# Hybrid DeltaNet and forgetting-attention trunk: later modulation strips, and an output projection whose second half gets its operands ahead of other loads

## The chip, the cores and the metric

The kernel runs on one core of a Trainium2 chip. The metric is the device time of one execution in microseconds (us).

## The reference

Two layers of width 1024 over 1024 tokens, in float32. Layer 0 mixes tokens by a gated delta rule (DeltaNet) with a short causal convolution, layer 1 by forgetting attention. Each layer normalizes its input and modulates it with a shift and a scale from a condition vector c; its result is multiplied by a gate, also from c.

```
cond = jax.nn.silu(c)
for i in range(DEPTH):                                   # DEPTH = 2
    mod = cond @ ada_w[i] + ada_b[i]                     # (1024) x (1024, 3072)
    shift, scale, gate = jnp.split(mod[:, None, :], 3, axis=-1)
    h = rmsnorm(x, norm_w[i]) * (1 + scale) + shift
    if i == 0:
        y = gdn_mixer(h, ...)     # input projection, conv, 16 heads of 128, ..., o @ w_out (2048 -> 1024)
    else:
        y = fox_mixer(h, ...)     # 16 heads of 64, softmax with a forget bias, gate, o @ w_out
    x = x + gate * y
return rmsnorm(x, final_norm_w)
```

## The kernel before

Float32 products are made from three matmuls on split operands: a rounded high part and the rest as low part (`mm3`; ScalarE writes the high part, VectorE or GpSimd subtracts for the low part). Tokens are in two halves of 512, and tiles of 128.

**The order of work.** TensorE's order is written out by hand. Generators (one for each strand of work) yield a delay, and a small planner, `Flow`, always advances the live one with the lowest priority number whose time has come; its clock adds the modelled cost of each matmul. What the other engines and the DMA queue do follows from the order in which work is emitted and from when its inputs and buffers are planned to be ready; each engine, and the queue on SyncE (SP) that issues all the DMAs here, then takes its list strictly in order. A tile of a pool is used again in rotation, and its next writer waits for the last reader.

**Layer 0** runs in 16 units, 8 groups of two heads for each token half (index `i`, `ts[i]`). A unit projects k, q and two v tiles and the z tiles (`proj_tile`), and then goes through the inversion of its triangular matrix (with DMA round trips through `lb`, `lr`, `rb` and `rmat`) and the chain of state updates. `done["kp"]` counts finished k tiles. Results go split to `og_d` and `ogl_d` in DRAM, 16 heads by 1024 tokens. In the units of the first half the weights are split and the parts stored to DRAM; in the second half most come back from there.

**Modulation strips.** The shift, scale and gate for layer 1, and the gate of layer 0, are made by `ada_all` in eight strips of 512 columns (`ada_strip`): eight loads of 128 x 512 into the two buffers `nx`, a multiply-add on VectorE for each, and a few matmuls into a bank of the ring `mm` (two PSUM banks, shared with the projections). `hold(lambda: done["kp"] >= AD0 + 1)` sets the unit with which they begin, and a copy of a piece of `ts[AD0]["k"]` into `nx` (L1283) ties the loads to that data.

**The output projection of layer 0** (`out_proj_a`) goes over token halves `h`, pairs of token tiles `tp`, column halves (in the first token half only) and 16 heads `k`. Weights come three steps ahead (`wnext`), are loaded to a third of `ht_h` (L433) and split to `whi` and `wlo`. The operands are read back from `og_d` and `ogl_d`, one head at a time (`ohi`, `olo`, L450, `out_o`), or, in the second token half after the first OX = 4 heads, two heads at a time (`yh`, `yl`, L461, `out_pair`), kept in the list `oq` in advance. The old x (`xs`, L507) is added at the end of a pair, and the new x is written to `x1_d` (L526).

**The second stage** begins, in the order of emission, when the chain of layer 0 is done: its memory takes the place of that of the units. While the second half of the projection runs, `norm2` goes through the eight token tiles (for the first four, x1 is read back into `v`, L1372, normalized into `wraw`, transposed on TensorE and split into `h2_h`, `h2_l`; the last four come from `n2read` without a reload), and `preload` fetches and splits the first eight weights of layer 1 through the buffer `kn` (L343). Then come attention and its output projection.

Of the kernel before, what the change touches and what calls it, by code (L numbers as in the profile page):

```python
# [8 lines left out]
F32 = mybir.dt.float32  # L9
# [9 lines left out]
KT = D // P  # L19
# [60 lines left out]
OGW = 2000  # L80
OL = 4
OX = 4
Y_NN = 8000
KPE = (7, 5)
KC = 3
# [3 lines left out]
Y_N2 = 8500  # L89
Y_N3 = 8500  # L90
ADP = 3500
AD0 = 5
R_AD = 600
R_AS = 2500
R_OA = 1150
# [100 lines left out]
def tile_trunk(  # L196
# [24 lines left out]
    nc = tc.nc  # L221
# [124 lines left out]
    def mm3(ps, wh, wl, ah, al, first, last):  # L346
        mm(ps, wh, ah, start=first, stop=False)
        mm(ps, wh, al, start=False, stop=False)
        mm(ps, wl, ah, start=False, stop=last)

    def hold(ok):
        while not ok():
            yield 300
# [10 lines left out]
    def xt_(shape, name, bufs=1, dt=F32):  # L364
        return px.tile(shape, dt, name=name, tag=name, bufs=bufs)

    xdone = {}
    where = {}

    wq, w_src, wcache = [], [], {}  # L370
    oq, o_src = [], []
# [19 lines left out]
    def oload(ahead):  # L391
        while len(oq) < ahead and o_src:
            oq.extend(o_src.pop(0)())

    def wnext(ahead):
        half(2)
        while len(wq) < ahead and w_src and len(set(wid)) < 3:
            wload()
        wid.pop(0)
        return wq.pop(0)  # L400
# [43 lines left out]
    def out_o(k, tok):  # L444
        def load():
            w = 2 * P
            hi = xt_([P, w], "ohi", 4, F32R)
            lo = xt_([P, w], "olo", 4, F32R)
            for v, d in ((hi, og_d), (lo, ogl_d)):
                nc.sync.dma_start(v.bitcast(F32), d[k, :, tok : tok + w])  # L450
            return [(hi, lo)]

        return load

    def out_pair(k, tok):
        def load():
            w = 2 * P
            pr = []
            for n, d in (("yh", og_d), ("yl", ogl_d)):
                v = where["py"].tile([P, 2, w], F32R, name=n, tag=n, bufs=4)  # L460
                nc.sync.dma_start(v.bitcast(F32), d[k : k + 2, :, tok : tok + w].rearrange("k p t -> p k t"))  # L461
                pr.append(v)
            return [(pr[0][:, i], pr[1][:, i]) for i in range(2)]

        return load

    def out_list(h):
        n = (512, D)[h]
        for tp in range(0, CPH, 2):
            for cs in range(0, D, n):  # L470
                w_src.extend(out_w(k, cs, n) for k in range(0, 16, D // n))
                if h:
                    k0 = 0 if tp else OX
                    o_src.extend(out_o(k, h * HALF + tp * P) for k in range(k0))
                    o_src.extend(out_pair(k, h * HALF + tp * P) for k in range(k0, 16, 2))
                else:
                    o_src.extend(out_o(k, tp * P) for k in range(16))

    def out_proj_a():
        gx = xt_([P, 4, D], "ht_h")  # L480
        gb0 = gx[:, 0]
        where["raw"] = [gx[:, i] for i in range(1, 4)]
        for h in range(2):
            n = (512, 1024)[h]
            if h:
                yield from hold(lambda: "bank" in where)
                yield OGW
            xs = xt_([P, CPH, D], "ht_l")
            for tp in range(0, CPH, 2):
                for cs in range(0, D, n):  # L490
                    acc = None
                    for k in range(16):
                        wh, wl = wnext((5, 3)[h])
                        if not h and (tp, cs, k) == (2, D - n, 8):
                            out_list(1)
                        oload((OL, 7)[h])
                        hi, lo = oq.pop(0)
                        if acc is None:
                            acc = []
                            for b in range(2 + 2 * h):  # L500
                                acc.append((yield from (acc_bank if b < 2 else where["bank"])()))
                        if (tp, cs, k) == (0, 0, 2):
                            if h == 0:
                                nc.sync.dma_start(gb0, gate_d[0:1, :].broadcast_to([P, D]))
                            for t in range(CPH):
                                r0 = (h * CPH + t) * P
                                nc.sync.dma_start(xs[:, t], x[r0 : r0 + P, :])  # L507
                        for t in range(2):
                            o = slice(t * P, (t + 1) * P)
                            for c in range(n // 512):  # L510
                                wc = slice(c * 512, c * 512 + 512)
                                mm3(acc[2 * c + t], hi[:, o], lo[:, o], wh[:, wc], wl[:, wc], k == 0, k == 15)
                            if h:
                                yield 0
                        if not h:
                            yield 0
                    for t in range(2):
                        for c in range(n // 512):
                            c0 = cs + c * 512
                            tg = xt_([P, D], "wlo", 5)[:, 0:512]  # L520
                            nc.vector.tensor_tensor(tg, acc[2 * c + t], gb0[:, c0 : c0 + 512], op=ALU.mult)
                            flow.free(acc[2 * c + t], R_OA + 600 * (2 * c + t))
                            xv = xs[:, tp + t, c0 : c0 + 512]
                            nc.gpsimd.tensor_tensor(xv, xv, tg, op=ALU.add)
                for t in range(tp, tp + 2):
                    nc.sync.dma_start(x1_d[h * CPH + t], xs[:, t])  # L526
                    if h:
                        where["n2read"](h * CPH + t, xs[:, t])
                    xdone[h * CPH + t] = flow.t

    with ExitStack() as sa:
# [133 lines left out]
        def norm_tile(xt, jk, evac, part=None):  # L665
# [4 lines left out]
            nc.vector.tensor_scalar(xt, xt, rs, None, op0=ALU.mult)  # L670
            yield Y_NN
            for k0 in range(0, KT, 4):
# [603 lines left out]
        def ada_all():  # L1276
            yield from hold(lambda: done["kp"] >= AD0 + 1)
            def al(shape, name, bufs):
                t = at([P, D], name, bufs) if name == "nx" else at([P, 512], name, bufs)
                return t[0 : shape[0], 0 : shape[1]]  # L1280

            for _ in range(2):
                nc.vector.tensor_copy(al([P, KT], "nx", 2), ts[AD0]["k"][:, 0, 0:KT])  # L1283
            for l, cl in strips:
# [26 lines left out]
    with ExitStack() as sb:  # L1311
# [3 lines left out]
        def bt(shape, name, bufs=1, dt=F32):  # L1315
            pool = pb if name in LEFT else where["p2"]
            return pool.tile(shape, dt, name=name, tag=name, bufs=bufs)
# [11 lines left out]
        h2_l = bt([P, KT, S], "h2_l", 1, F32R)  # L1329
        sy = sb.enter_context(ExitStack())  # L1330
        where["py"] = sy.enter_context(tc.tile_pool(name="py", bufs=1, reuse_waits="tile"))

        def small(sh, n, b=1):
            return pb.tile(sh, F32, name=n, tag=n, bufs=b)
# [27 lines left out]
        def norm2(t):  # L1362
            yield from hold(lambda: t in xdone)
            if t >= CPH:
                yield max(0.0, xdone[t] + Y_N3 + 2500 * (t % 2) - flow.t)
                hf = bt([P, KT, P], "v", 4)
                jk = n2jk[t]
            else:
                yield 2500
                hf = bt([P, KT, P], "v", 4)  # L1370
                xt = hf.rearrange("p k t -> p (k t)")
                nc.sync.dma_start(xt, x1_d[t])  # L1372
                yield 1500
                jk = [bt([P, 512], "wraw", 2) for _ in range(2)]
                scaled(xt, jk)
                yield Y_N2
            for k0 in range(0, KT, 4):
                ps = yield from pst("pt", 2)
                for k in range(4):
                    tr_(ps[:, k * P : (k + 1) * P], jk[k0 // 4][:, k * P : (k + 1) * P], ident)  # L1380
                for k in range(4):
                    kk = k0 + k
                    nc.vector.tensor_scalar(
                        hf[:, kk], ps[:, k * P : (k + 1) * P], gcol[1][:, kk : kk + 1],
                        scol[1][:, kk : kk + 1], op0=ALU.mult, op1=ALU.add,
                    )
                flow.free(ps, R_N)
                yield 0
            tok = slice(t * P, (t + 1) * P)
            split(h2_h[:, :, tok], h2_l[:, :, tok], hf)  # L1390
# [19 lines left out]

        def preload():
            raw = bt([P, 2, 512], "kn")
            for k in range(KT):
                yield Y_PB
                bload(raw[:, k % 2])
# [528 lines left out]
```

## Time and profile before

| | |
|---|---|
| time, median of 3 runs | 1947.3 us (1943.26 to 1947.73) |
| the profiled execution | 1945.78 us, span 1943.8 us |
| granted TensorE clock, mean | 0.971 |
| busy: PE, PE weight load | 1828.4 us (94%), 1524.4 us (78%) |
| busy: DVE, ACT, POOL | 1328.3 us (68%), 1033.3 us (53%), 367.0 us (19%) |
| bytes moved by DMA | 307.16 MB, mean 158 GB/s |
| loads of the strips | 64 of 256 KB, 3.4 us to landing, from 325.7 to 754.0 us |

PE is TensorE's matmuls, PEld its weight loads, DVE VectorE, ACT ScalarE, POOL GpSimd, SP the engine that issues DMAs (SPq its queue). A row of a timeline gives the start in us, the length, the engine, the line of the kernel, the operation, and what it writes from what. In square brackets stands the idle time of that engine just before and what ended it. A row of waits gives the total in us, how often, and the longest. Matmuls are pipelined and their ends are modelled, so two starts tell more than one length. The granted clock is given as a share of full speed.

### The profile page before, as it was taken

To read this page: it belongs to the slowest core of one execution; us is meant where nothing else is said; L and a number is where in the kernel's file an instruction comes from. 1 tells how busy PE (TensorE), PEld (TensorE's weight loads), DVE (VectorE), ACT (ScalarE), POOL (GpSimd) and SP (SyncE) were. 2 spreads that over 40 slices of the span, in tenths; PEclk is the share of its full clock that TensorE was granted. 3 is DMA by queue.
4 is the path that set the end of the run, shared out by engine and by line. 5 is a ranking of instruction groups with operands and counts; after the bars stand their busy time and mean duration, and the time that the engine had idled before them with its cause. 6 is when DMAs were issued, how large, how long until landed. Compare 5 with 4: busy or idle time off the path is not lost.

```text
span 1943.8 us, 35877 instructions
## 1 busy us (share of the span) xinstructions
PE 1828.4 (94%) x12888; PEld 1524.4 (78%) x12888; DVE 1328.3 (68%) x3323; ACT 1033.3 (53%) x2674; POOL 367.0 (19%) x402
## 2 busy tenths in 40 slices
PE   6989999999899999999899799999999999999798
PEld 4767778777787878878776578798988988989576
DVE  5677888788786777776665585475665656656764
ACT  4565566565564555555444453465565555655631
POOL 1100110101210110010001244223223132221222
PEclk7889999899999999999999899999999999999899
DMA  7576767667656565454689982112021011112423
GB/s 270 187 229 205 233 210 245 207 212 249 229 181 186 173 192 176 148 172 138 206 268 320 356 303 98 31 48 66 24 65 60 23 60 45 44 55 71 155 87 95
DMA packets 224985, 307.16 MB, mean 158 GB/s; under 512 B 100460, under 2 KB 136940, under 8 KB 224808
## 3 DMA queue, kind: packets, MB, share of 16 engines
q1 hardware_dynamic: 223800, 304.65, 48.4%
q8 instruction: 101, 1.65, 0.4%
q14 instruction: 76, 0.62, 0.1%
q10 hardware_dynamic: 1008, 0.23, 0.1%
HBM read 223.15 MB, written 81.67 MB: 157 GB/s over the span
## 4 chain that ended last, share of the span: by engine, by line
PE 62%; DMA 14%; DVE 13%; ACT 4%; issue 3%; POOL 1%; SPq 1%; ACTq 0%; DVEq 0%; POOLq 0%
PE mm L137 39%; PE lg L137 5%; PE su L137 4%; PE pt L141 3%; PE oT L137 3%; DMA nx<-in_ada_w_dram 3%; PE tr L141 3%; PE ch L137 2%; DVE wlo L340 2%; PE co L137 2%; DVE cv_y L833 2%; DMA ohi<-og_d 2%; DMA rmat<-rb 1%; DMA wraw<-in_wb_dram 1%; ACT whi L337 1%
## 5 line engine op out<-in xcount | busy, mean ns | idle before, releaser
L137 PE MATMUL mm<-ht_h,whi 128*128 128x512 f32 x768 | 342.4, 446 | 0.5 <-DVE nh L313 0.5
L137 PE MATMUL mm<-ht_h,wlo 128*128 128x512 f32 x768 | 305.2, 397 | 0.0
L137 PE MATMUL mm<-ht_l,whi 128*128 128x512 f32 x768 | 304.3, 396 | 0.8 <-POOL ht_l L340 0.8
L137 PE MATMUL mm<-whi,h_h 128*128 128x384 f32 x512 | 186.7, 365 | 0.9 <-DVE kn L1533 0.9
L137 PE MATMUL mm<-wlo,h_h 128*128 128x384 f32 x512 | 172.6, 337 | 0.6 <-POOL wlo L340 0.6
L137 PEld LDWEIGHTS mm<-ht_h,wlo 128*128 128x128 f32 x768 | 146.3, 190 | 33.9
L137 PE MATMUL mm<-whi,h_l 128*128 128x384 f32 x512 | 172.7, 337 | 0.0
L1684 DVE TENSOR_TENSOR ptl<-pt,pth 128x512 fp32r<-128x512 f32 x192 | 106.4, 555 | 92.5 <-ACT pth L1683 90.5
L137 PEld LDWEIGHTS mm<-ht_h,whi 128*128 128x128 f32 x768 | 147.2, 192 | 28.4 <-issue 1.7
L137 PEld LDWEIGHTS mm<-ht_l,whi 128*128 128x128 f32 x768 | 147.7, 192 | 25.2 <-POOL ht_l L340 1.2
L1683 ACT CAST pth<-pt 128x512 fp32r<-128x512 f32 x192 | 91.3, 477 | 139.8 <-PE pt L141 139.0
L833 DVE SCALAR_TENSOR_TENSOR cv_y<-cv_t,conv_h,cv_y 128x512 f32<-128x512 f32 x192 | 144.4, 752 | 17.3 <-ACT cv_y L825 15.6
L1648 ACT ACTIVATE lg<-lg,mx 128x896 f32<-128x896 f32 (+7 forms) x128 | 99.5, 777 | 54.3 <-DVE mx L1640 48.6
L1527 POOL TENSOR_TENSOR rs<-ss,mhalf 128x4 f32<-128x4 f32 x64 | 64.5, 1007 | 330.8 <-DVE ss L1525 325.2
L340 DVE TENSOR_TENSOR wlo<-ht_h,whi 128x512 fp32r<-128x512 f32 x124 | 93.3, 792 | 47.3 <-ACT whi L337 45.1
L337 ACT CAST whi<-ht_h 128x512 fp32r<-128x512 f32 x124 | 70.7, 618 | 86.5 <-PE mm L137 38.6
L137 PE MATMUL mm<-h_h,whi 128*128 128x512 f32 x240 | 100.5, 419 | 0.7 <-DVE wlo L1783 0.3
L137 PEld LDWEIGHTS mm<-whi,h_h 128*128 128x128 f32 x512 | 97.8, 191 | 3.5 <-ACT v L1529 1.2
L137 PEld LDWEIGHTS mm<-wlo,h_h 128*128 128x128 f32 x512 | 97.2, 190 | 2.8 <-POOL wlo L340 0.8
L141 PE MATMUL pt<-ident,lg 128*128 128x128 f32 (+1 forms) x584 | 96.0, 273 | 3.1 <-ACT lg L1648 3.1
L137 PEld LDWEIGHTS mm<-whi,h_l 128*128 128x128 f32 x512 | 96.4, 188 | 0.0
L137 PE MATMUL mm<-h_h,wlo 128*128 128x512 f32 x240 | 94.9, 395 | 0.0
(390 smaller groups left out, 4492.9 us busy)
## 6 DMA issues: line engine op xcount, KB each, us to landing
ht_h<-in_wa_o_dram SPq DMA_DIRECT2D x62, 512.0 KB, 5.2
wc<-whi SPq DMA_DIRECT2D x45, 512.0 KB, 4.5
wc<-wlo SPq DMA_DIRECT2D x45, 512.0 KB, 4.3
wlo<-wc SPq DMA_DIRECT2D x45, 512.0 KB, 4.9
whi<-wc SPq DMA_DIRECT2D x45, 512.0 KB, 3.6
wlo<-in_wa_c_dram SPq DMA_DIRECT2D x35, 512.0 KB, 4.3
nx<-in_ada_w_dram SPq DMA_DIRECT2D x64, 256.0 KB, 3.4
wraw<-in_wb_dram SPq DMA_DIRECT2D x56, 256.0 KB, 2.8
```

The costliest lines, as they stand in the source:

```text
L137: self.nc.tensor.matmul(out, lhsT, rhs, start=start, stop=stop)
L141: self.nc.tensor.transpose(out, src, ident)
L337: nc.scalar.copy(hi, src)
L340: (lo_eng or nc.gpsimd).tensor_tensor(lo, src, hi.bitcast(F32), op=ALU.subtract)
L833: nc.vector.scalar_tensor_tensor(y, raw[:, j : j + HALF], w[:, j : j + 1], y, op0=ALU.mult, op1=ALU.add)
L1527: nc.gpsimd.tensor_tensor(rs, ss, mhalf[:, 0:4], op=ALU.pow)
L1648: nc.scalar.activation(lg, lg, AF.Exp, scale=-1.0, bias=mx[:, hh : hh + 1], accum_out=sums[:, tt : tt + 1],)
L1683: nc.scalar.copy(ph_[:, cs], pp[:, cs])
L1684: nc.vector.tensor_tensor(pl_[:, cs], pp[:, cs], ph_[:, cs].bitcast(F32), op=ALU.subtract)
```

## The change

Three things change.

1. `AD0` goes from 5 to 9, so that the strips begin with the tenth unit and not with the sixth.
2. When the second stage is set up, up to OX + 2 * YF = 10 operands of the projection's second half are asked for at once (four are there, so three pairs of two heads are added).
3. Loads beside the second half are tied to its own progress. `where["kno"]` counts its steps of 16 heads (two pairs of token tiles, 32 steps), and `where["late"]` is the low part of the weight of the latest step. The old x is loaded at the tenth step of the first pair and not at the third; the four x1 reloads of `norm2` wait for steps 6, 9, 12 and 15; `preload` waits for step 13. Before each such load a GpSimd copy of 8 columns of that weight is written into the load's destination, so that the load itself can't start before this weight has been split. There are ten such copies.

```
-AD0 = 5
+AD0 = 9
+YF = 3
+KN2 = (6, 9, 12, 15)
+KPL = 13
...
@@ out_proj_a, in the loop over the 16 heads k
-                        if (tp, cs, k) == (0, 0, 2):
+                        if h:
+                            where["late"] = wl
+                            where["kno"] = where.get("kno", 0) + 1
+                        if (tp, cs, k) == (0, 0, 2 + 7 * h):
                             if h == 0:
                                 nc.sync.dma_start(gb0, gate_d[0:1, :].broadcast_to([P, D]))
                             for t in range(CPH):
                                 r0 = (h * CPH + t) * P
+                                if h:
+                                    nc.gpsimd.tensor_copy(xs[:, t, 0:KT], wl[:, 0:KT].bitcast(F32))
                                 nc.sync.dma_start(xs[:, t], x[r0 : r0 + P, :])
@@ second stage, after its pools for h2_h, h2_l and yh, yl
+        for n_pair in range(8):
+            if o_src and len(oq) < OX + 2 * YF:
+                oq.extend(o_src.pop(0)())
@@ norm2, the first four token tiles
-                yield 2500
+                yield from hold(lambda: where.get("kno", 0) >= KN2[t])
                 hf = bt([P, KT, P], "v", 4)
                 xt = hf.rearrange("p k t -> p (k t)")
+                nc.gpsimd.tensor_copy(xt[:, 0:KT], where["late"][:, 0:KT].bitcast(F32))
                 nc.sync.dma_start(xt, x1_d[t])
                 yield 1500
@@ preload
             raw = bt([P, 2, 512], "kn")
+            yield from hold(lambda: where.get("kno", 0) >= KPL)
+            for v in range(2):
+                nc.gpsimd.tensor_copy(raw[:, v, 0:KT], where["late"][:, 0:KT].bitcast(F32))
             for k in range(KT):
                 yield Y_PB
                 bload(raw[:, k % 2])
```

The function inside `out_pair` is also given the name `load_pair`; nothing tests for that name.

More of the change, by code (lines that the diff above doesn't have):

```diff
@@ L455, in out_pair, with load_pair @@
     def out_pair(k, tok):
-        def load():
+        def load_pair():
             w = 2 * P
@@ L463, in load @@
             return [(pr[0][:, i], pr[1][:, i]) for i in range(2)]
-        return load
+        return load_pair
     def out_list(h):
```

## The prediction

> **What bounds the kernel now.** I read the busy time by stage first, cut at the events of the change: the sixth and the tenth unit of the gated DeltaNet layer, the start of its output projection (945), that projection's second half (1079 to 1192), and the attention layer. Columns: stage, its length, busy PE, PE's weight loads, DVE, ACT, POOL (instructions), granted clock, DMA share, GB/s.
>
> ```profile
> 240.00:325.00 85.00, 83.05 (x798) 67.35 (x791) 68.21 (x208) 56.31 (x170) 8.40 (x18) 1.00 0.67 209
> 325.00:560.00 235.00, 219.13 (x1928) 177.82 (x1927) 192.49 (x473) 139.53 (x414) 33.86 (x47) 0.96 0.68 221
> 560.00:760.00 200.00, 193.57 (x1735) 157.65 (x1734) 152.29 (x414) 104.31 (x320) 20.36 (x28) 0.99 0.62 191
> 760.00:945.00 185.00, 183.32 (x1663) 149.73 (x1661) 130.37 (x377) 100.93 (x318) 16.86 (x24) 1.00 0.45 139
> 945.00:1079.00 134.00, 122.75 (x759) 96.53 (x758) 77.36 (x144) 60.78 (x149) 12.43 (x9) 0.96 0.91 301
> 1079.00:1192.00 113.00, 99.01 (x431) 78.95 (x430) 80.16 (x141) 51.93 (x98) 40.48 (x28) 0.94 0.81 288
> 1192.00:1944.00 752.00, 722.17 (x4118) 630.56 (x4117) 453.25 (x1136) 389.62 (x858) 202.39 (x178) 0.99 0.19 61
> ```
>
> TensorE sets the time nearly everywhere: what can be won is its idle time and its slow clock. Idle is length less busy: 15.9 us in 325-560, 6.4 in 560-760, 1.7 in 760-945, 11.3 in 945-1079, 14.0 in 1079-1192. From 945 to 1192 the DMA engines are nearly full (0.91, 0.81), so there the order of transfers matters. Next, who TensorE waits for, first in 1080-1200, then, with its longest entry, in 325-560.
>
> ```profile
> PE mm L137 <- DMA yh<-og_d: 9.6, 1, 9.6
> PE pt L141 <- DVE wraw L1353: 2.1, 1, 2.1
> PE mm L137 <- DMA yl<-ogl_d: 1.5, 1, 1.5
> ...
> PE su L137 <- DVE tmat L1223: 3.6, 4, 2.2
> ```
>
> In the second half one wait is most of the idle time: the first pair of operands, yh. The DMA queue's timeline shows why it is late.
>
> ```profile
> 1081.29 0.32 SPq L1142 DMA_DIRECT2D ogl_d<-ogl  x1
> 1085.02 0.44 SPq L1372 DMA_DIRECT2D v<-x_d  x1
> 1086.18 0.33 SPq L343 DMA_DIRECT2D kn<-in_wb_dram  x1
> ...
> 1092.07 0.33 SPq L1430 DMA_DIRECT2D fb<-in_f_bias_dram  x1
> 1093.35 0.38 SPq L461 DMA_DIRECT2D yh<-og_d  x1
> ...
> 1089.35 0.39 PE L137 MATMUL lg<-whi,olo 128*128 128x512 f32 x1
> 1099.33 0.76 PE L137 MATMUL mm<-whi,yh 128*128 128x512 f32 x1 [9.59 <-DMA yh<-og_d]
> ```
>
> TensorE has used up the four small operands by 1089.7. yh is issued only at 1093.35, behind reloads of x1 (v) and weights of the next layer (kn), and lands after 6 us.
>
> **The change, part by part.** The sum is made against the profiled execution, 1945.78 us (span 1943.8), which is 1.5 below the median of 1947.3.
>
> 1. Modulation strips start at the tenth unit. Eight strips, each of eight loads of 256 KB and a sum, are moved whole. Their old and new starts (the k tile of the sixth and of the tenth unit), and the matmul that closes the first and the last strip:
>
> ```profile
> 324.77 0.69 DVE L840 SCALAR_TENSOR_TENSOR k<-cv_t,cv_y 128x512 f32<-128x512 f32 x1 [0.16 <-ACT cv_t L837]
> 325.69 0.33 SPq L279 DMA_DIRECT2D nx<-in_ada_w_dram  x1
> 380.10 0.59 PE L137 MATMUL mm<-nh,ones 128*1 128x512 f32 x1
> 561.38 0.69 DVE L840 SCALAR_TENSOR_TENSOR k<-cv_t,cv_y 128x512 f32<-128x512 f32 x1
> 789.95 0.59 PE L137 MATMUL mm<-nh,ones 128*1 128x512 f32 x1
> ```
>
> A strip takes (789.95 - 380.10) / 7 = 58.5 us, the first 54.4. From 562 the first ends at about 616, the sixth at 909 (its modulation is read only after 1080, so no one waits), the seventh at 967, the eighth at 1026. So four strips leave 325-560, 560-760 has four in both kernels, three come into 760-945 and one, with the tail of another, into the first half of the projection.
>
> What leaves: in 325-560 SP waits inside the strips' loads while the round trips of the triangular inverse stand behind them, and DVE, busy 192.5 of 235, waits in its turn.
>
> ```profile
> SPq L279 <- DVE nh L286: 14.1, 18, 3.1
> SPq L279 <- DMA nx<-in_ada_w_dram: 10.6, 7, 3.5
> ...
> 406.63 0.33 SPq L279 DMA_DIRECT2D nx<-in_ada_w_dram  x1
> 409.95 1.97 SPq L1153 DMA_DIRECT2D lb<-d  x4
> 415.96 2.78 SPq L1157 DMA_DIRECT2D lr<-lb  x4
> 420.55 0.18 DVE L1167 TENSOR_TENSOR xtmp<-lr,xi 128x15 f32<-128x15 f32 x1 [4.05 <-DMA lr<-lb]
> ```
>
> Bounds: the stage before, without strips, idles 1.95 in 85 us at full clock, which makes 5.4 in 235. Against it, 325-560 loses 15.9 idle and 0.04 x 235 = 9.4 of clock: at most 25.3 - 5.4 = 19.9 is the strips', at least 0. The stage also holds the change to the second token half with a load of its own, and its waits are on DVE results that other work delays too, so I take half of the idle surplus (5.2) and a third of the clock: -8.
>
> What comes: 560-760, with strips, idles 6.4 per 200 against 1.7 per 185 in 760-945: (0.0322 - 0.0091) x 185 = 4.3, with the clock (0.01) 6.1 at most, 0 at least; a gain is excluded, as this stage has next to no idle time to give. I take +3. In 945-1079 the eighth strip brings 2.1 MB, at 301 GB/s 7.0 us, all hidden or none: +3. Both strips also ask for one of the two PSUM banks that the projection holds for 16 steps at a time; at a group's end the strip's two matmuls and its copy then stand between two groups. Rows: matmuls twice 0.59, copy 0.67 (the group below), some 1.9 a strip, 0 to 3.8 for both: +2. This part in all: 0.
>
> ```profile
> L313 DVE COPY nh<-mm x4: 669/671/671, 381.5 to 791.8; 1x512 f32<-1x512 f32 x4
> ```
>
> 2. Three operand pairs are asked for as soon as the second stage's memory exists, ahead of v and kn. Six DMAs of 256 KB come earlier, none is added. The earliest place is behind ogl_d at 1081.3; the landing of 6 us then gives 1087 to 1088, before 1089.7. If the memory is free only when the last og_d write has landed (kn's issue at 1086.18 ended that wait) it is 1092. Stall 0 to 2.5 in place of 9.6: I take 1.5, -8.1. After the wait the clock is low:
>
> ```profile
> 1090.00:1100.00 10.00, 0.67 (x2) 0.60 (x3) 3.94 (x9) 4.43 (x10) 2.60 (x3) 0.69 1.04 399
> 1100.00:1110.00 10.00, 8.61 (x34) 6.62 (x32) 5.04 (x14) 4.15 (x9) 0.74 (x2) 0.80 1.04 394
> 1150.00:1160.00 10.00, 7.90 (x33) 6.16 (x32) 8.60 (x22) 3.69 (x9) 1.61 (x3) 0.83 0.98 334
> ```
>
> 0.20 x 10 = 2.0 us in 1100-1110; half of it, -1.0, as a short stall may stay. The yl wait of 1.5 goes as well, as these operands now lead: -1.5.
>
> 3. x of the second half, x1 of four norm tiles, and the next layer's first weights wait for late weights. Ten POOL copies of 8 columns are added (nearest row, POOL's 3-column copy, 229 ns): 2.3 us of POOL, hidden by its 72 idle us in 1079-1192. The transfers themselves, 2 + 2 + 2 MB, go from 1085-1121 to later steps, of 12 matmuls each:
>
> ```profile
> 1112.57 0.40 PE L137 MATMUL mm<-whi,yh 128*128 128x512 f32 x1
> 1115.37 0.40 PE L137 MATMUL mm<-whi,yh 128*128 128x512 f32 x1
> L831 POOL COPY cv_t<-halo 128x3 f32<-128x3 f32 x32 | 7.3, 229 | 167.3 <-DVE k L840 39.9 <-DVE xi L1171 38.3 <-DVE q L840 38.2
> L340 POOL TENSOR_TENSOR h_l<-v,h_h 128x1024 fp32r<-128x1024 f32 x8 | 20.1, 2509 | 13.1 <-ACT h_h L337 13.1
> 1142.66 0.42 SPq L1372 DMA_DIRECT2D v<-x_d  x1
> DMA to landing us min/median/max: 8.3/8.6/8.9
> ```
>
> A step is 2.8 us, so x at step ten of 32 has some 17 us to the adds that need it, and the eight weights from step thirteen are due only at 1192: both free. The norm tiles are the tight ones. v takes 8.6 us to land (last row), and the order written out leaves 10 us of matmul time, about 11 real, between load and transposes. Before, three tiles were loaded early (the first at 1085.02, above); the fourth only at 1142.66, and it is the 2.1 us wait on wraw above, with a clock of 0.83 behind it (1.7 us). If all four run like that, three more cost 3 x 3.8 = 11.4; if the late weights are ready a step or two ahead, 0 (and the old 3.8 could go too, the lower end). I am nearer to the low end, as the split of a weight is done before its step: +3. By the Trainium skill, TensorE: Matmul & The Clock Gate, "What's actually happening", the clock halves after at least one idle window of about 3.4 us. By that rule such waits cost 2.1 each and I would put +2; the row of 1150-1160 after a wait of 2.1 disagrees, and I stay with it.
>
> Sum: 0 - 8.1 - 1.0 - 1.5 + 3 = -7.6, so 1945.8 - 7.6 = 1938.
>
> **The rivals.** (a) Slower: the ties hold up SP. A tied load waits on SP for a POOL copy, this for POOL's work ahead, and the projection's weights and operands queue behind. Priced at one h_l split (2.5 us) for each of ten ties: 25 in place of 3, so 1960. It decides against the change from about 1.8 us a tie (18 in all, past 1953). For it: SP takes its queue in order, as yh showed. Against: three weights are prefetched, over 8 us of cover. By the Trainium skill, SBUF - State Buffer, "shared port pair", a GpSimd operation locks some DVE operations out for its whole length, so the later norm work would also stretch on DVE; the slowest of the eight scalings below fits one h_l split, the median shows it to be rare. Chance 0.12.
>
> ```profile
> L1353 DVE TENSOR_SCALAR wraw<-v,ln_rs x8: 475/484/2625, 1095.7 to 1154.3; 128x512 f32<-128x512 f32 x8
> ```
>
> (b) The late strips land in the full DMA queue: both strips' 4.2 MB exposed (14.0) and 3.8 for banks instead of 5: 12.8 more, 1951. For it: 0.91 DMA share. Against: TensorE still was busy 92% there. Chance 0.12.
>
> (c) The change does not do what it says: yh stays behind, because its memory comes free late or the queue is full (issues stand 1.2 us apart). Then 9.1 is lost: 1947. For it: kn's wait on og_d. Against: at 1085 the queue did take v. Chance 0.12.
>
> (d) The strips were nearly all of the loss in 325-560: -19.9 for -8, 1926. For it: the granted clock is 1.00 before and after that stage. Chance 0.13.
>
> **How the numbers follow.** The forecast has 0.51, with a range of its own from 1932 to 1945. Within 0.3% of the median, about what a measurement of this kernel can tell from no change, is 1941.5 to 1953.1. Faster: 0.42 of the forecast and (d), 0.55. Slower: (a) and 0.02 of (b), 0.14. Same: the rest, 0.31. The range 1925 to 1953 leaves out (a) and the lower edge of (d).
>
> **What would show it.** Right: no wait on yh above 2.5 us; yh issued within 5 us of the last ogl_d; second half under 106 us (113 now); 325-560 idle near 10 us with a clock of 0.98; first half no longer than 139. Wrong: waits of PE on wraw or the weights' splits in the second half over 6 us together, SP waiting on POOL's small copies for more than a microsecond each, or the strip's loads beside waits on ohi after 990.

## The result

The change makes the kernel slower: median 1960.86 us (1953.04 to 1965.35, six runs) against 1946.5 us for before on the same chip, a ratio of 1.0070 [1.0050, 1.0089]. The profiled execution took 1953.04 us (span 1951.3, mean granted clock 0.974), 7.3 us more than before's 1945.78. It is the fastest of the six, so its trace holds only half of the loss of the medians.

The stages of after, cut as before (length, busy PE, PE's weight loads, DVE, ACT, POOL, granted clock, DMA share, GB/s):

```profile
325.00:560.00 235.00, 226.28 (x1995) 185.58 (x1995) 180.32 (x470) 147.84 (x437) 31.67 (x50) 0.99 0.62 199
560.00:760.00 200.00, 186.76 (x1763) 150.28 (x1762) 150.62 (x403) 98.42 (x307) 16.36 (x25) 0.97 0.59 178
760.00:945.00 185.00, 175.10 (x1520) 144.24 (x1519) 135.67 (x373) 94.09 (x300) 16.55 (x24) 0.97 0.55 171
945.00:1079.00 134.00, 125.12 (x777) 96.69 (x775) 84.71 (x155) 59.89 (x149) 11.75 (x8) 0.99 0.87 295
1079.00:1192.00 113.00, 100.80 (x436) 77.69 (x436) 82.85 (x144) 55.79 (x104) 48.87 (x37) 0.98 0.87 309
1192.00:1944.00 752.00, 727.95 (x4138) 635.47 (x4136) 454.29 (x1134) 388.57 (x856) 203.16 (x177) 0.99 0.19 61
```

The stage that the strips left idles 8.7 us where it idled 15.9, and its clock rose from 0.96 to 0.99. The next two idle 13.2 and 9.9 where they idled 6.4 and 1.7, and their clock fell from 0.99 and 1.00 to 0.97. Fixed cuts drift when a kernel runs late, so the table goes by events: the k tiles of units 6, 10, 14 and 16, the last evacuation of each projection half, and the last matmul. Each entry is the time between two such rows of the profiled execution, in us. One execution of a kernel differs from the next: the last column, where nearly the same work runs in all of them, goes from 739.5 to 746.9. The runs below the first two are told of later.

| | units 6-10 | 10-14 | 14-16 | to the end of the first half | second half | rest |
|---|---|---|---|---|---|---|
| before | 236.6 | 223.1 | 107.1 | 186.0 | 114.9 | 743.4 |
| after | 221.2 | 234.4 | 118.2 | 188.0 | 110.7 | 745.5 |
| e1, strips moved alone | 221.4 | 237.1 | 118.0 | 188.3 | 117.8 | 739.5 |
| e2, projection alone | 234.2 | 224.5 | 106.5 | 185.8 | 112.2 | 746.9 |
| e18, strips nearly empty | 217.4 | 225.6 | 107.1 | 187.0 | 116.0 | 742.1 |
| e9, loads without the sums | 220.5 | 231.9 | 112.4 | 192.1 | 116.2 | 742.4 |
| e13, strips at the ninth unit | 226.0 | 229.1 | 113.9 | 189.0 | 120.4 | 742.2 |
| e14, the same, an eighth of the bytes | 221.6 | 225.1 | 111.8 | 185.6 | 118.6 | 741.9 |
| e15, before, an eighth of the bytes | 228.8 | 231.3 | 106.0 | 186.2 | 113.1 | 743.0 |
| e6, before, four slices | 233.1 | 237.3 | 107.0 | 186.1 | 117.2 | 743.2 |

After against before: -15.4, then +11.3 and +11.1, +2.0, -4.2 and +2.1. The relief is there, and units 10 to 16 take back one and a half times as much.

TensorE's waits from 561 to 890, in before and then in after (total, times, longest):

```profile
PE tr L141 <- ACT rmat L1218: 2.7, 2, 1.6
PE tr L137 <- DVE ogt L1133: 2.0, 1, 2.0
PE ch L137 <- DVE state L1095: 1.0, 2, 0.8
```

```profile
PE ch L140 <- DVE state L1103: 8.4, 6, 3.3
PE su L140 <- DVE tmat L1256: 3.9, 2, 2.9
PE tr L144 <- ACT rmat L1226: 3.5, 2, 1.9
PE ch L140 <- DVE xp L1058: 2.1, 1, 2.1
```

The wait that grew most is that for the state, VectorE's last step of a chain, from 1.0 to 8.4. All of units 10 to 16, in before and then in after:

```profile
561.38:891.58 330.20, 322.10 (x2898) 261.97 (x2897) 243.25 (x679) 175.73 (x546) 34.20 (x48) 0.99 0.57 176
545.79:898.43 352.64, 332.08 (x2920) 270.57 (x2919) 260.14 (x705) 176.38 (x556) 31.27 (x48) 0.98 0.58 179
```

TensorE idles 8.1 us there in before and 20.6 in after, and the waits for the state are 7.4 of the 12.5 that came on top. Its clock stood at half for 3.4 us in before and, behind the three waits of more than 2 us (2.9, 2.1 and 3.3), for 17.1 us in after, at most 6.8 us of lost time more. Together that is 19.3 of the 22.4; for the rest I have no row.

The longest wait for the state in after's timeline, VectorE first, then the matmul that waits:

```profile
794.49 0.75 DVE L289 SCALAR_TENSOR_TENSOR nh<-nx,cond,nh 128x512 f32<-128x512 f32 x1 [1.44 <-DMA nx<-in_ada_w_dram]
...
795.50 1.89 DVE L983 SCALAR_TENSOR_TENSOR d<-su,wn,d 128x128 f32<-128x128 f32 x7
797.31 0.74 DVE L289 SCALAR_TENSOR_TENSOR nh<-nx,cond,nh 128x512 f32<-128x512 f32 x1
797.97 0.60 DVE L1103 SCALAR_TENSOR_TENSOR state<-state,g_ex,co 128x128 f32<-128x128 f32 x2
...
798.71 0.67 PE L140 MATMUL ch<-state,k 128*128 128x256 f32 x2 [3.31 <-DVE state L1103]
```

A strip's multiply-add (nh) waits 1.44 us for its load, with everything behind it, and a second one stands right ahead of the state update. Between 545 and 895 such multiply-adds start between the end of the matmul that the update needs (co) and the update at 4 of 24 updates in before and at 7 of 23 in after. There are also more of them in that stretch: 28 in before, 42 in after.

In the second half of the projection, TensorE's waits in after:

```profile
PE mm L140 <- ACT whi L340: 3.9, 2, 2.8
PE mm L140 <- DVE wlo L343: 2.8, 5, 1.3
PE pt L144 <- DVE wraw L1364: 2.4, 2, 1.6
PE lg L140 <- DVE wlo L529: 1.4, 1, 1.4
```

No operand is waited for any more. The splits of the weights (whi and wlo, L340 and L343) are, 6.7 us in all. The wlo of L529 is no split but the product with the gate, written to a buffer of that name: there TensorE waits 1.4 us for a PSUM bank to be read out.

### The profile page after: what moved, and what is told of

Its sections match the earlier page's. It is cut to its first block, busy times and chain, and to the rows that moved or that the text cites. A ratio compares the mean times of both kernels' runs of the same rounds, so it can differ in the third digit from the quotient of the medians.

```text
span 1951.3 us, 35911 instructions
## 1 busy us (share of the span) xinstructions
PE 1831.3 (94%) x12888; PEld 1524.7 (78%) x12888; DVE 1332.6 (68%) x3323; ACT 1031.7 (53%) x2674; POOL 369.5 (19%) x412
## 4 chain that ended last, share of the span: by engine, by line
PE 58%; DVE 15%; DMA 15%; ACT 6%; issue 3%; SPq 2%; POOL 1%; ACTq 0%; DVEq 0%; POOLq 0%
PE mm L140 37%; PE lg L140 4%; PE su L140 3%; PE oT L140 3%; PE pt L144 3%; DMA nx<-in_ada_w_dram 3%; DVE wlo L343 3%; PE tr L144 2%; DMA ht_h<-in_wa_o_dram 2%; PE ch L140 2%; DVE cv_y L841 2%; DMA ohi<-og_d 2%; DMA rmat<-rb 1%; PE co L140 1%; ACT whi L340 1%
## 5 line engine op out<-in xcount | busy, mean ns | idle before, releaser
L343 DVE TENSOR_TENSOR wlo<-ht_h,whi 128x512 fp32r<-128x512 f32 x124 | 96.0, 810 | 56.3 <-ACT whi L340 53.3
L1542 POOL TENSOR_TENSOR rs<-ss,mhalf 128x4 f32<-128x4 f32 x64 | 64.5, 1008 | 331.4 <-DVE ss L1540 328.7
L340 ACT CAST whi<-ht_h 128x512 fp32r<-128x512 f32 x124 | 70.7, 618 | 85.8 <-DMA ht_h<-in_wa_o_dram 39.4
```

Of the source, the lines that this page charges most:

```text
L340: nc.scalar.copy(hi, src)
L343: (lo_eng or nc.gpsimd).tensor_tensor(lo, src, hi.bitcast(F32), op=ALU.subtract)
L1542: nc.gpsimd.tensor_tensor(rs, ss, mhalf[:, 0:4], op=ALU.pow)
```

## The experiments

Ratios are medians against runs of before on the same chip. The theories of the expectations: 1, the strips' multiply-adds wait in VectorE's queue ahead of work of the units; 2, the tied loads hold SyncE's queue; 3, the bytes of the strips' loads crowd the DMA engines; 4, SyncE stands at a strip's load until its buffer is free, and weights and round trips queue behind ("widened": VectorE's waits for the load count as well); 5, the order of SyncE's and VectorE's instructions, which the build writes out anew for each edit, decides.

**The two parts alone.** e1 is before with `AD0 = 9`; e2 is after with `AD0 = 5`; e8 is before with only the early request of three operand pairs:

```
+        for n_pair in range(8):
+            if o_src and len(oq) < OX + 2 * YF:
+                oq.extend(o_src.pop(0)())
```

e1: 

> The kernel before with AD0 = 9 alone: the strips begin with the tenth unit, nothing else changes. Theory 1 (a strip costs time wherever it runs, because its multiply-adds wait for their loads in VectorE's queue and the state updates of the chain stand behind them; late units suffer more): the whole slowdown is here, 1955 to 1964, from the sixth to the tenth k tile some 15 us less, from the tenth to the sixteenth some 22 us more, and the spread over the runs is as wide as that of the changed kernel. Theory 2 (the tied loads of the projection hold up SyncE's queue): at most 1948, and the loss is in the other half of the change.

e2: 

> The changed kernel with AD0 = 5: only the edits around the second half of the output projection. Theory 1: 3 to 6 us faster than before, 1941 to 1944, the yh wait of 9.6 us gone, and the spread over the runs as narrow as that of the kernel before. Theory 2: 1955 or more.

e8: 

> The kernel before with the early request for three operand pairs alone, without the ties: x, x1 and the next weights are loaded as before. If the ties cost what the early operands win (waits on the weights' split of 2.7, 1.3, 2.9 and 3.9 us stand where the yh wait was), this is 4 to 8 us faster than before, 1938 to 1942. If the three pairs only push the same bytes around, it is the same as before within 3 us, and the second half still takes 112 to 115.

Measured: e1 1.0076 [1.0053, 1.0099], e2 1.0004 [0.9987, 1.0020], e8 1.0008 [0.9992, 1.0024]. The whole loss comes from the strips; the projection's part is worth nothing that can be measured. The end of the first half to the end of the program takes 858.3 us in before, 856.2 in after, 859.1 in e2: what the second half saves is not seen at the end. Theory 2 falls, as the ties stand in e2.

**Multiply-adds or loads.** With `AD0 = 9`, e3 keeps of each strip's eight multiply-adds the first and the last, e4 keeps two of the eight loads.

```
-                else:
+                elif k == KT - 1:        # e3
...
+                if kk < 2:               # e4; else w = ws[kk - 2]
```

e3: 

> The strips begin with the tenth unit (as in the first kernel of this set), all their loads are made, but of the eight multiply-adds of a strip only the first and the last are kept, so the modulation is not the reference's. Theory 1: 20 to 30 us less than with the strips moved alone, some 1930 to 1940, as nothing waits for the loads in VectorE's queue any more. Theory 3 (it is the traffic of the loads, or SyncE held by them): within 5 us of the kernel with the strips moved alone.

e4: 

> The strips begin with the tenth unit, all multiply-adds are made, but only the first two loads of a strip, whose data the later ones use again, so the modulation is not the reference's. Theory 1 in its waiting form (the adds cost because they wait): 15 to 25 us less than with the strips moved alone. If the adds cost by VectorE's own time (6 us a strip), at most 5 us less. Theory 3 (traffic): 20 us less here, and nothing in the kernel without the adds.

Measured: e3 1.0086 [1.0059, 1.0113], e4 0.9994 [0.9977, 1.0011]. The multiply-adds by themselves are not the loss, so theory 1 falls in that form; the loads are needed for it. e3 is not clean, though: with no reader between them, a load waits for the landing of the one before it in its buffer, and SyncE stands:

```profile
SPq L279 <- DMA nx<-in_ada_w_dram: 79.9, 36, 5.6
```

**SyncE's stand at the loads.** Each nx buffer of 128x1024 gets two rows of 512 in place of one (four slices), with the strips at the tenth unit (e5) and at the sixth (e6). In e7 the strips, at the tenth unit, are loaded from GpSimd's queue.

```
+                    if not pair:
+                        v = at([P, D], name, bufs)
+                        pair.extend([v[:, 0:512], v[:, 512:D]])
+                    t = pair.pop(0)
...
-                nc.sync.dma_start(w, ada_w[...])
+                nc.gpsimd.dma_start(w, ada_w[...])        # e7
```

e5: 

> The strips alone begin with the tenth unit, and the two buffers of their loads, of which half was unused, hold two rows each, so four loads can be under way and SyncE waits less for a free buffer; bytes and sums are unchanged. Theory 4 (SyncE stands at a strip's load until a buffer is free, and the weights and the inversion's round trips queue behind): most of the 14 us come back, 1944 to 1950. Theory 3 (the bytes crowd the DMA engines): no change, 1956 to 1963.

e6: 

> The kernel before with the same four slices, strips from the sixth unit. Theory 4: the loss of 15 us that the strips cause between the sixth and the tenth k tile shrinks too, 1932 to 1941. Theory 3: as before, 1943 to 1947.

e7: 

> The strips alone begin with the tenth unit, and their loads are issued from GpSimd's queue, so SyncE never stands at one; GpSimd does. Bytes, buffers and sums are unchanged. Theory 4: 1944 to 1952, if GpSimd's own small steps of the chain are not held in turn. Theory 3: 1956 or more.

Measured: e5 1.0045 [1.0026, 1.0065], e6 1.0072 [1.0046, 1.0097], e7 1.0080 [1.0058, 1.0102]. e5 may get back a part (its interval overlaps that of e1), e7 nothing, and e6 loses where it should have had less to wait for. SyncE's stand is not needed for the loss, as e7 has it without that; VectorE still waits 17.8 us for the loads there (561 to 890). e6 loses 14 us in units 10 to 14, most of it in one place. Its SP queue, VectorE and TensorE there:

```profile
579.43 1.80 SPq L1153 DMA_DIRECT2D lb<-d  x4
...
584.22 1.91 SPq L1157 DMA_DIRECT2D lr<-lb  x4
586.18 2.80 SPq L1177 DMA_DIRECT2D rb<-xi  x4
590.29 1.78 SPq L1184 DMA_DIRECT2D rmat<-rb  x4
...
582.36 0.17 DVE L1171 TENSOR_TENSOR xi<-xi,xtmp 128x8 f32<-128x8 f32 x1
...
592.47 0.29 PE L137 MATMUL su<-tmat,d 16*32 16x16 f32 x2 [7.98 <-DVE tmat L1194]
```

Two round trips overlap. The older one has its xi at 582.5, but its rb stands in SP's order behind lr of the younger, which waits for lb to land, and goes out at 586.18. TensorE idles 8.0 us and then runs at a granted clock of 0.50 from 590 to 600. The order of TensorE's instructions is the same as in before; SP's and VectorE's are not. SP's order in all these kernels: e6 and e4 have this inversion, both at this trip; before, after, e1, e3 and e7 do not. e4's unit 10 took 68.5 us with a wait of 6.8, where e1 has 59.0, so its 0.9994 contains about 10 us that do not belong to the question. e5 has half of the inversion, two of the four rb behind lr:

```profile
566.53 0.89 SPq L1177 DMA_DIRECT2D rb<-xi  x2
567.66 1.90 SPq L1157 DMA_DIRECT2D lr<-lb  x4
569.60 0.98 SPq L1177 DMA_DIRECT2D rb<-xi  x2
```

Its unit 10 took 64.5 us with a wait of 3.8, 5.5 us more than e1's, so some 0.3 of its 0.45 per cent may be the inversion's, and what four slices are worth at the tenth unit stays open.

**The order put right, and the loads alone.** e11 is e6 with a pace of 3600 for 3500, by which the order is the old one again. e9 is e5 without the six inner multiply-adds: all loads, and hardly a wait of VectorE for them. e10 and e12 are e5 and e6 with each multiply-add two paces behind its load.

```
-ADP = 3500
+ADP = 3600                                             # e11
...
-    al, acc_bank, l, cl, 512, ("nx", 2), ("nh", 2), ("nh", 2), 1, ADP
+    al, acc_bank, l, cl, 512, ("nx", 2), ("nh", 2), ("nh", 2), 2, ADP    # e10, e12
```

e11: 

> The strips stay at the sixth unit with four slices, as in the run that came out at 1.0072 of before, and their pace goes from 3500 to 3600. In that run the four rb transfers of the tenth round trip stand behind the lr transfers of the next one in SyncE's order, two of the four after the first, and its unit 10 took 67 us with 8 us of idle TensorE where before has 58; with 3600 the order is the old one again. Theory 5 (the order written out at build decides): unit 10 back to about 58 us, the time 0.997 to 1.001 of before. If four slices cost for another reason: it stays at 1.005 to 1.009.

e9: 

> The strips move to the tenth unit, their buffers hold two rows each, so that a load waits for no buffer, and of a strip's eight multiply-adds only the first and the last are done (the modulation is not the reference's). All 64 loads are still made, and hardly any instruction waits for one. Theory 3, the bytes crowd the DMA engines: as slow as with the strips alone, 1956 to 1960 beside 1944 for before, and units 10 to 16 take 350 us or more. Theory 4 widened, the loads cost only through the queues that stand waiting for them (SyncE for a buffer, VectorE for the data): units 10 to 16 about 335, the time 1935 to 1945. Theory 5, the order written out at build around unit 10 decides: the time goes by that unit alone, 58 us or 67.

e10: 

> The strips at the tenth unit with two rows in a buffer (four slices), and each multiply-add two paces behind its load in place of one. The computation is whole. If VectorE's waits for a slice are the other half of the loss (theory 4 widened), its waits for the loads go from some 18 us to under 5 and the time from 1.0045 of before to 0.998 to 1.001 of it. If it is the bytes (theory 3), it stays at 1.004 to 1.008.

e12: 

> The strips at the sixth unit, four slices, each multiply-add two paces behind its load, pace 3500; the round trips' order in SyncE's queue is the old one. The computation is whole. Theory 4 widened: the strips' cost of some 15 us in units 6 to 10 and 10 us in units 10 to 14 shrinks by a third, the time 0.993 to 0.998 of before. Theory 3 (the bytes): 0.999 to 1.001. Theory 5: anything within 0.7 per cent on either side, by what the order does to single units.

Measured: e11 0.9990 [0.9973, 1.0008], e9 1.0054 [1.0034, 1.0075], e10 1.0062 [1.0041, 1.0084], e12 1.0012 [0.9994, 1.0030]. e11 shows that a tenth of a microsecond of planned pace, by the order that it gives, is worth 0.8 per cent. TensorE's own order changes with the pace too, so the trip is not changed alone; but unit 10 takes 55.0 us where e6 takes 67.2, and that is 12.2 of the 15.8 us between their profiled executions. Its queue at the same trip has rb first:

```profile
564.89 1.80 SPq L1177 DMA_DIRECT2D rb<-xi  x4
...
572.15 1.83 SPq L1153 DMA_DIRECT2D lb<-d  x4
...
577.71 1.90 SPq L1157 DMA_DIRECT2D lr<-lb  x4
```

In e9 the loads cost without most of the multiply-adds. VectorE waits 17.9 us for the round trips' lr from 561 to 890 (longest 6.7), and the median lb takes 3.9 us to land; with nearly empty strips (e18, below) it is 9.5 and 1.8 (the wait and the landing of e9, then of e18; the landing from 545 to 890):

```profile
DVE xtmp L1167 <- DMA lr<-lb: 17.9, 5, 6.7
```

```profile
lb<-d SPq DMA_DIRECT2D x24, 32.0 KB, 3.9
```

```profile
DVE xtmp L1170 <- DMA lr<-lb: 9.5, 6, 2.9
```

```profile
lb<-d SPq DMA_DIRECT2D x24, 32.0 KB, 1.8
```

The change does not show this, though. The same wait for lr in before and then in after:

```profile
DVE xtmp L1167 <- DMA lr<-lb: 8.9, 5, 2.7
DVE xtmp L1175 <- DMA lr<-lb: 6.6, 5, 2.3
```

It is shorter in after, and the median lb lands in 1.8 us in before, 2.6 in after and 3.8 in e11, which is as fast as before. Nor are the loads of e9 without waits: with no reader between them, SP stands at them as in e3 (from 545 to 890; in after it is 20.0 us, 15 times).

```profile
SPq L279 <- DMA nx<-in_ada_w_dram: 25.8, 18, 5.7
```

e10 waits 4.2 us for its loads on VectorE, after 18.6 and e5 8.4, and is no faster than e5; but both have the half inversion (e10's unit 10 took 65.6 us), and TensorE's order differs between them. Clearer are e11 and e12 at the sixth unit, with the regular order: from 320 to 790 VectorE waits 8.7 and 8.5 us for the loads where before waits 20.2, and neither is faster than before. At the old place these waits are worth nothing that can be seen.

**Place, phase and bytes.** e13 and e17 start the strips at the ninth and eighth unit (`AD0 = 8`, `7`). e16 is e1 with the pace of 3600. e14 (ninth unit) and e15 (sixth) load an eighth of each slice:

```
+    nc.sync.dma_start(w[:, 0:64], ada_w[layer, kk * P : (kk + 1) * P, col : col + 64])
```

e13: 

> The kernel before with the strips one unit earlier than in the change (they start after the ninth unit's keys). Computation whole. It is the yardstick for the next kernel. Theory 3 (bytes) has no reason for another cost than at the tenth unit: 1.005 to 1.009 of before. Theory 5 (what the order around single units happens to be) allows 0.996 to 1.009, and a value under 1.003 would speak for it.

e14: 

> As the strips after the ninth unit, and each of the 64 loads brings 64 of its 512 columns, which the multiply-add reads eight times over (the modulation is not the reference's). The count of the loads and of the multiply-adds, their waits and their places in the queues' order stay nearly the same; the bytes fall to an eighth, from 16.8 to 2.1 MB. Theory 3 (the bytes crowd the DMA engines): 10 to 25 us faster than with full loads, some 1930 to 1938. Theory 4 (the queues that stand for a transfer): a short transfer lands sooner as well, half of that, 1940 to 1948. Theory 5: no more than 0.3 per cent from the run with full loads.

e15: 

> The kernel before, strips at the sixth unit, each load an eighth as above (the modulation is not the reference's). It measures what the bytes cost at the old place. Theory 3 with the profiles' stage times (the strips there cost about 15 us in units 6 to 10 and some 10 in units 10 to 14): 1922 to 1935. If the old place is cheap because the bytes cost nothing there: 1940 to 1946.

e16: 

> The strips at the tenth unit as in the change, their pace 3600 in place of 3500; bytes, counts, buffers and place are the same, only the phase of the loads against the units moves, and with it the order written out at build. Computation whole. Theories 3 and 4: 1.005 to 1.009 of before, as with 3500. Theory 5: it moves by more than 0.3 per cent, most likely down, to 0.999 to 1.004.

e17: 

> The strips after the eighth unit's keys; computation whole. So far the loss grows with the place: sixth unit 1.000 (before), ninth 1.0028, tenth 1.0076. If the place decides (the later they start, the more of them stand in units 14 to 16 and in the projection's first half, where before has no strip load): 0.998 to 1.002. If the phase against the pairs of units decides (odd units against even): it can be as slow as the tenth, 1.005 or more.

Measured: sixth unit 1 (before), eighth 1.0050 [1.0032, 1.0067], ninth 1.0028 [1.0008, 1.0048], tenth 1.0076, tenth with the other pace 1.0086 [1.0065, 1.0107]. An eighth of the bytes: at the ninth unit 0.9995 [0.9979, 1.0012], at the sixth 1.0003 [0.9985, 1.0020]. At the ninth unit, where both kernels have the regular order, the bytes are thus worth about 0.3 per cent, the whole of its loss against before. (A short load also lands sooner, so this does not part the bytes from the waits for them.) At the sixth nothing is seen of them in the time, but its trace has 7.8 us less in units 6 to 10 and a wait of 6.2 in unit 10, with two of the four rb late as in e5. e16 says that the tenth unit's loss is not an accident of one pace. From the sixth to the tenth the loss does not simply grow with the place: the eighth and the ninth have the other order, by intervals that just overlap. No kernel that does the whole computation beats before; the lowest is e11, with 1 inside its interval.

**Nearly empty strips.** e18 has the strips at the tenth unit with one load and one multiply in place of eight:

```
+                if kk < 1:               # else w = ws[0]
...
-                else:
+                elif k == KT:            # never
```

> The strips at the tenth unit with one load and one multiply each in place of eight of both (the modulation is not the reference's); their closing matmuls, banks and pace stay. It shows what the kernel takes with next to nothing of the strips' work, while the round trips' order in SyncE's queue is the old one. If what the strips cost at the old place (some 15 us in units 6 to 10, and up to 10 in units 10 to 14) is theirs and adds up: 1918 to 1930. If the relief is given back elsewhere, by a lower clock or by other waits, whatever the strips do: 1938 to 1946.

Measured: 1929.69 us, 0.9935 [0.9916, 0.9955], and it shows what each stage takes with next to none of the strips' work:

```profile
325.00:560.00 235.00, 226.88 (x2024) 187.04 (x2024) 185.46 (x486) 150.04 (x447) 30.97 (x50) 1.00 0.62 203
560.00:760.00 200.00, 194.05 (x1808) 157.66 (x1807) 136.42 (x386) 105.87 (x335) 18.52 (x28) 0.97 0.48 146
760.00:945.00 185.00, 183.50 (x1728) 151.09 (x1727) 132.14 (x360) 99.41 (x307) 14.89 (x21) 1.00 0.48 152
```

In units 6 to 10 neither e18 nor after, e1 and e9 have any strip, and they took 217.4 and 220.5 to 221.4: these 4 us are not a cost of strips (TensorE idles 8.1 to 9.4 us in each). By the table, then, the strips' work costs before 15 to 19 us in units 6 to 10 (236.6 less 221.4 or 217.4), and nothing in units 10 to 14 (223.1 against 225.6), where its other four strips stand. Moved to the tenth unit (e1) it costs 11.5, 10.9 and 1.3 in the second to fourth columns. By the medians all of it is worth 0.65 per cent, 13 us, at the sixth unit, and 1.0076 - 0.9935 = 1.4 per cent, 27 us, at the tenth, if the little that e18 keeps costs the same at both places. With an eighth of the bytes but all loads and multiply-adds, e14 and e15 are still 0.6 and 0.7 per cent above e18 (e15 with its half inversion): the bytes are the smaller part of the price.

## Why the prediction was wrong

**The step that failed** is "What comes" in part 1: +3 with a bound of 6.1 for the strips in 560-945. It measured +22.4 (11.3 + 11.1), 19.4 more; the whole sum was 14.9 too low against the profiled execution (-7.6 forecast, +7.3 measured), so this term is more than all of the miss. The price was read off before's 560-760, which held four strips and idled 4.3 us more than the stage behind it. e18, with nearly empty strips, idles 6.0 us from 560 to 760, as much as before's 6.4, and takes no less time for units 10 to 14: this stage lost nothing that can be seen to its strips, so the row could give no price. The same units took 11.3 more in after, when four other strips stood there. So the cost of a strip could not be carried from one stage to the next; that it depends on which instruction of the units stands behind its loads and multiply-adds is my reading of the timelines, not shown by a run. The bound of 6.1 failed with the price, since it came from the same row: a stage with little idle time has all of it still to lose.

What makes up the 27 us is shown in part. It needs the loads (e4). In after's own trace most of the added idle time is the wait for the state (7.4 of 12.5 us), and the clock behind the longer waits comes on top; the wait of 2.9 us on tmat stands in e18 too and so is not the strips'. But the wait for the state is not what has to be there: e9 has a quarter of the multiply-adds and 2.1 us of it, and still costs 1.0054 against 0.9935, which is 23 us, by other waits (17.9 us of VectorE's for lr, 25.8 of SP's at the loads). e7 has SP's stand taken away and costs as much as e1. So taking away one wait at a time left the loss, and which path carries it, the bytes or the queues that stand for them, stays open. Why the same bytes cost nothing visible in before's units 10 to 14 stays open: the phase and the order differ, and no run here held both and moved the place alone.

**Relief in 325-560**, -8 with bounds to -19.9: it was -15.4, and e18 finds 15 to 19 of the strips' work there. The bounds held; taking half of the idle surplus and a third of the clock was too careful. Rival (d) had this mechanism right and its 1926 wrong, since it left the other terms alone.

**First half, banks.** +3 and +2: the first half took +2.0 with one wait of 1.00 us on a strip's copy, and its waits on operands (ohi and olo) were 8.1 us against 10.4. Rival (b) is out; that half was not where it went wrong.

**Operands first**, -10.6 in all: yh was issued at 1085.97, 6.0 us after the last ogl_d at 1080.01, and nothing waits for it; the clock from 1090 to 1110 is 1.00 where it was 0.69 and 0.80. So the mechanism is right, though yh came 1.0 us later than the sign named for it. The sum is wrong, because I did not ask what is late next: the splits of the weights (6.7 us) and wraw (2.4), together more than the 6 us named as a sign against it. The second half became 110.7 and not under 106; the rest of the program was 2.1 longer, which is within its spread. e2 and e8 put the worth of it at 0.

**Ties**, +3: the wait on wraw, which this term priced, is 2.4 us in two where it was 2.1 in one. SP waited three times for the copy into v on GpSimd, 3.0 us in all with 1.4 the longest, once 1.0 for that of kn and once 0.6 for that of the old x. Rival (a) has its mechanism with 4.6 us of SP's waits where it priced 25.

**Clock.** By the Trainium skill, TensorE: Matmul & The Clock Gate, "What's actually happening", it takes an idle window of about 3.4 us to halve the clock. In after a wait of 2.9 us was enough for 0.73 over the following ten, in which TensorE was busy throughout:

```profile
580.00:590.00 10.00, 7.09 (x119) 5.83 (x118) 7.11 (x29) 9.30 (x34) 1.10 (x1) 0.93 0.48 145
590.00:600.00 10.00, 10.00 (x54) 8.12 (x53) 5.01 (x9) 0.58 (x1) 2.03 (x3) 0.73 0.21 59
```

That is 2.7 us behind a wait of 2.9, so the prediction's price for a wait and the clock behind it (3.8 for 2.1) was about right, and the rule disagrees with this row. So do the other short waits told of in the last section.

## What to carry to other kernels

The cost of background work is not read from a stage that carries it today: a stage that runs well with it may run badly with the same kind of work begun at another time, so a cheap first experiment is to run with that work nearly empty, which tells what each stage takes without it. Read a stage's difference beside that of a stage which the work never touched (4 us here). Where the build orders in-order queues anew after each edit, compare the orders of two kernels before explaining their times: one trip's write-back behind the next trip's read took some 9 to 12 us in one unit here (e6 against before and against e11), and half of that order some 5, in runs meant to test something else. And when a wait is removed in front of a queue of prepared operands, price what is second in line.

## What the runs showed of the hardware

A transfer of 32 KB (lb) took 1.8 us to land, by the median from 545 to 890, in e18, which has few loads of 256 KB beside it, 1.8 in before with 30 of them, 2.6 in after with 50, 3.4 in e7 with 50 on another queue, and 3.9 in e9 with 56. The mean DMA shares from 561 to 890 are 0.49, 0.57, 0.57, 0.58 and 0.59: the share of a stage says little about the delay of a small transfer. The trace tells the landing of only some of these transfers (5 of 24 in e9, 3 in after, 9 in e18), so the medians are rough.

The clock fell behind short waits. In before and in after together TensorE has twelve waits of more than 2.0 us between 250 and 1195, of 2.1 to 9.6 us, and behind each the trace shows a granted clock of 0.50 for 3.4, 6.8 or 10.2 us. Four of after's are of 2.1, 2.5, 2.8 and 2.9 us. It is not so without exception: e9 and e18 have a wait of 3.2 us near 400 with no such stretch behind it. e6's wait of 8.0 us was followed by 0.50 up to the 600th us and beyond:

```profile
590.00:600.00 10.00, 6.43 (x77) 5.31 (x78) 6.65 (x31) 2.28 (x8) 0.29 (x1) 0.50 0.09 15
```

TensorE works 6.43 us of these ten, from 592.47 on, at half its clock, so about 3.2 us came on top of the wait.
